# Two matmuls per head, from stacked high and low parts, in the second block's attention

## The chip, the cores and the metric

One Trainium2 chip, one core. The metric is device time in microseconds of the whole program, the median of several executions. PE is TensorE (matmuls), PEld its weight loads, DVE VectorE, ACT ScalarE, POOL GpSimd, SP the engine that issues most DMAs.

## What is computed

A first block (an MLA layer, an RG-LRU layer, each followed by a SwiGLU) on 272 tokens, then a second block of two layers on 256 tokens with model width 2048. The change touches only the attention of the second block. Each of its layers has 32 heads of 64 channels in four kinds of mixer, eight heads each, cut here to what matters:

```python
h = rms_norm_2(x, norm_gain[layer])
proj = jnp.einsum('bsd,dc->bsc', h, w_in[layer])          # q, k, v, gate, forget
o_a = dilated_attention(rope(norm(q[0])), rope(norm(k[0])), v[0])
o_b = stick_breaking_attention(q[1], k[1], v[1])
o_c = moba_attention(rope(norm(q[2])), rope(norm(k[2])), v[2])
o_d = forgetting_attention(norm(q[3]), norm(k[3]), v[3], log_f)
y = heads_side_by_side(o_a, o_b, o_c, o_d) * silu(gate)
x = x + jnp.einsum('bsc,cd->bsd', y, w_out[layer])
```

For each head this is: scores q.k over 256 queries and 256 keys (the upper triangle is masked out), a softmax or the stick-breaking weights, and the product of these weights with the values.

## The kernel before, in words

All matmuls take operands of type float32r. To keep float32 precision, an operand x is split into a high part (x cast to float32r on ACT) and a low part (x minus the high part, on DVE), and `mm3` (L225) makes a product of three matmuls: high by high, high by low, low by high. `wblock` (L206) does the same to each block of weights that a DMA on SP brings in (`wraw`): ACT casts `wh` (L216), DVE subtracts `wl` (L191). Several such blocks are in flight.

`block2` (L685) runs the four mixers of a layer in the order 1, 0, 2, 3. Per mixer there are four pairs of heads, i = 0 to 3. `values` (L714) projects v for two pairs at once; `qkg` (L738) projects q, k and the gate of one pair, and `qk` (L823) normalizes, rotates and splits q and k (channels of the pair's two heads on partitions 0 to 63 and 64 to 127, the 256 tokens as columns). `attend` (L759) does the attention of one pair, so it is called 16 times per layer, 32 times in all: 8 times with `stick` (L921) and 24 times with `soft` (L881). `out_proj` (L777) of the previous mixer is put between.

Both `soft` and `stick` work on two blocks of 128 queries (`lo`, `hi`). A matmul contracts over all 128 partitions, that is over both heads at once, so one of the two operands must be block-diagonal. `diag` (L871) copies a block of 128 columns into such a form, [head 0 | 0; 0 | head 1], 256 columns wide, into buffers that `diagpad` (L860) has zeroed once per layer; POOL copies the high part, DVE the low part, two casts each (L878). With it the scores of the first block take one `mm3` of 256 columns for both heads (L896 in `soft`, L931 in `stick`), those of the second one `mm3` of 256 columns for each head (L902, L930):

```python
qd = self.diag(q, hi)
kd = self.diag(k, lo)
self.mm3(s0[:, 0:256], (q[0][:, lo], q[1][:, lo]), kd, NC is None, True)
for j in range(2):
    s = s1[:, j * 256:j * 256 + 256]
    self.mm3(s, block(qd, j), (k[0][:, 0:256], k[1][:, 0:256]), NC is None, ...)
```

The value product (L767, L768) loads the values of both heads, 128 columns, and streams the attention weights of both heads, 512 columns for the first 128 keys and 256 for the others; of the result o (128 x 512) each head takes its own half of the partitions, multiplied by the gate (`yt`, L773), which is then split into `yh` (L774) and `yl`.

The order in which each engine does its work is set when the program is built, by the framework's scheduler from the data dependences and the program's order; PE fills waits of one attention with projections of another part. Tiles come from pools with a fixed number of buffers, 66 in the large pool "s".

Of the kernel before, what the change touches and what calls it, by code (L numbers as in the profile page):

```python
# [9 lines left out]
F32 = mybir.dt.float32  # L10
F32R = mybir.dt.float32r
# [43 lines left out]
def halves(x, n):  # L55
    return x.rearrange("p (j c) -> p j c", c=n)


def block(pair, j):
    return [t[:, j * 128:j * 128 + 128] for t in pair]  # L60

# [14 lines left out]
class Net:  # L76
# [608 lines left out]
    def block2(self, l, st, rb, first_done, after):  # L685
# [24 lines left out]
        NC = None  # L710
        self.diagpad(4)
        Y = {}

        def values(mx, hf):  # L714
            out = []
            ft = []
            c = 264 if mx == 3 and hf == 0 else 256
            src = a[f"vf{l}"] if c == 264 else a[f"v{l}"][(1, 0, 2, 3).index(mx) * 2 + hf - (mx == 3)]
            ws = [self.wblock(src[b], 8 * c, 4 * c) for b in range(2)]
            for tt in range(2):  # L720
                p = self.ps()[:, 0:c]
                ts = slice(tt * 128, tt * 128 + 128)
                for k in range(KD):
                    xh, xl = X[k]
                    self.mm3(p, (xh[:, ts], xl[:, ts]), self.wcol(ws[k // 8], (k % 8) * c, c), k == 0, k == KD - 1)
                if c == 264:
                    ft.append(self.small.tile([128, 8], F32, tag="ft", name="ft"))
                    nc.vector.tensor_scalar(ft[tt], p[:, 256:264], rcol()[:, tt:tt + 1], None, ALU.mult)
                p = p[:, sl]
                vh = self.slot("vh", F32R)[:, sl]  # L730
                vl = self.slot("vl", F32R)[:, sl]
                rc = rcol()[:, tt:tt + 1]
                nc.scalar.activation(vh, p, AF.Copy, scale=rc)  # L733
                nc.vector.scalar_tensor_tensor(vl, p, rc, vh.bitcast(F32), ALU.mult, ALU.subtract)
                out.append((vh, vl))
            return out, ft
# [22 lines left out]
        def attend(mx, i, q, k, g, v):  # L759
            o = self.pa("o2")  # L760
            c = slice((i % 2) * 128, (i % 2) * 128 + 128)
            hv = [[t[:, c] for t in x] for x in v]
            if mx == 1:
                p0, p1 = self.stick(q, k, masks)
            else:
                p0, p1 = self.soft(q, k, masks, NC if mx == 3 else None, i)
            self.mm3(o, hv[0], p0, True, False)  # L767
            self.mm3(halves(o, 256)[:, :, 128:256], hv[1], p1, False, True)  # L768
            yh, yl = Y[mx][i]
            t = self.slot("yt", tag="a")[:, sl]  # L770
            for j in range(2):
                R = slice(j * 64, j * 64 + 64)
                nc.vector.tensor_tensor(t[R], o[R, j * 256:j * 256 + 256], g[R], ALU.mult)  # L773
            nc.scalar.copy(yh, t)  # L774
# [48 lines left out]
    def qk(self, l, mx, qk, p, rb):  # L823
# [4 lines left out]
        if mx == 1:  # L828
            if qk == 0:
                nc.vector.scalar_tensor_tensor(t, p, 0.125, rb()[:, sl], ALU.mult, ALU.mult)  # L830
            else:
                nc.vector.tensor_tensor(t, p, rb()[:, sl], ALU.mult)
            return self.split(t, "qk", n)
        nc.vector.tensor_tensor(t, p, rb()[:, sl], ALU.mult)
# [21 lines left out]
        if mx == 3:  # L856
            return self.split(t, "qk", n)
        return self.rope(t, self.b2const["rope2c"], self.b2const["rope2s"], n, "qk", (v, y))

    def diagpad(self, n):  # L860

        self.dp = []
        self.dpi = 0
        for _ in range(n):
            pr = (self.slot("dph", F32R), self.slot("dpl", F32R))
            for t in pr:
                for j in range(2):
                    self.nc.gpsimd.memset(t[j * 64:j * 64 + 64, 128 - j * 128:256 - j * 128].bitcast(F32), 0.0)
            self.dp.append(pr)

    def diag(self, x, c):  # L871

        pr = self.dp[self.dpi % len(self.dp)]
        self.dpi += 1
        for t, s, eng in zip(pr, x, (self.nc.gpsimd, self.nc.vector)):
            for j in range(2):
                R = slice(j * 64, j * 64 + 64)
                eng.tensor_copy(t[R, j * 128:j * 128 + 128], s[R, c])  # L878
        return [t[:, 0:256] for t in pr]

    def soft(self, q, k, masks, NC, i):  # L881
# [3 lines left out]
        lo, hi = slice(0, 128), slice(128, 256)  # L885
        qd = self.diag(q, hi)
        kd = self.diag(k, lo)
        if NC is not None:
# [6 lines left out]
            nc.tensor.matmul(s1, self.one, nb, start=True, stop=False)  # L895
        self.mm3(s0[:, 0:256], (q[0][:, lo], q[1][:, lo]), kd, NC is None, True)  # L896
        P = []
        for j in range(2):
            P.append([self.softmax(s0[:, j * 128:j * 128 + 128], 128, 128, masks[0])])
        for j in range(2):  # L900
            s = s1[:, j * 256:j * 256 + 256]
            self.mm3(s, block(qd, j), (k[0][:, 0:256], k[1][:, 0:256]), NC is None, NC is None or j == 1)  # L902
        for j in range(2):
# [17 lines left out]
    def stick(self, q, k, masks):  # L921
# [4 lines left out]
        lo, hi = slice(0, 128), slice(128, 256)  # L926
        qd = self.diag(q, hi)
        kd = self.diag(k, lo)
        for j in range(2):
            self.mm3(z0[:, j * 256:j * 256 + 256], block(kd, j), (q[0][:, 0:256], q[1][:, 0:256]))  # L930
        self.mm3(z1[:, 0:256], (k[0][:, hi], k[1][:, hi]), qd)  # L931
        Z, SP = [], []
# [279 lines left out]
```

## Time and profile before

| | us |
|---|---|
| median of 3 executions | 3184.17 |
| lowest and highest | 3183.94, 3185.53 |
| profiled execution | 3183.68 |
| its span, from the first to the last instruction | 3181.9 |
| PE busy | 3159.5 |
| DVE busy | 2160.8 |
| ACT busy | 1758.9 |
| POOL busy | 588.9 |

A busy time is the union of the durations of an engine's instructions. Matmuls overlap, so what PE takes for one is read from the distance of the starts. In the rows a group is named by its line, its engine, its operation, what it writes and reads and the shapes; 128*128 is the size of the loaded weights, behind it stand the output's partitions and columns.

### The profile page before, as it was taken

Reading aid. Unit: us, or ns where it says so; the run is one execution under the profiler, and the core shown is the slowest. Engines: PE = TensorE matmul, PEld = TensorE weight load, DVE = VectorE, ACT = ScalarE, POOL = GpSimd, SP = SyncE. Lnnn points to the kernel's source line nnn. Section 1 sums busy time; section 2 is a strip of 40 time slices with the busy share of each in tenths; the row PEclk is TensorE's granted clock in tenths of the full one; section 3 lists DMA queues with packets and bytes.
Section 4 is the critical chain, followed back from the end, with each engine's and each line's share of the span. In section 5 each row is a group of like instructions: output and inputs, shape, how many; then the busy total and the mean of one; then the engine's idle time right before and its main releaser. Section 6 shows DMA issues by size and latency. Waiting matters only on the chain.

```text
span 3181.9 us, 64455 instructions
## 1 busy us (share of the span) xinstructions
PE 3159.5 (99%) x25987; PEld 3139.0 (99%) x25987; DVE 2160.8 (68%) x3673; ACT 1758.9 (55%) x2970; POOL 588.9 (19%) x730
## 2 busy tenths in 40 slices
PE   9999999999999999999999999999999999999999
PEld 9999999999999999999999999999999999999999
DVE  7887655555555678865555555578788778778876
ACT  6765434434344567754444444456677666666764
POOL 1001000000000134310000000023244463144453
PEclk9999999999999999999999999999999999999999
DMA  6344556556565555566565656556555555555554
GB/s 226 118 131 127 179 158 194 175 160 190 160 191 170 178 176 171 166 194 187 173 201 171 204 182 189 189 165 201 167 166 164 175 159 177 160 174 169 167 168 134
DMA packets 165693, 549.43 MB, mean 173 GB/s; under 512 B 18800, under 2 KB 38128, under 8 KB 165392
## 3 DMA queue, kind: packets, MB, share of 16 engines
q1 hardware_dynamic: 163440, 540.70, 54.6%
q8 instruction: 203, 3.33, 0.4%
q0 software_dynamic: 1664, 4.33, 0.4%
q14 instruction: 98, 0.80, 0.1%
q10 hardware_dynamic: 288, 0.27, 0.0%
HBM read 543.13 MB, written 2.10 MB: 171 GB/s over the span
## 4 chain that ended last, share of the span: by engine, by line
PE 83%; DVE 2%; issue 1%; DMA 1%; POOL 1%; ACT 1%; POOLq 0%; ACTq 0%; DVEq 0%; SPq 0%
PE p L230 27%; PE p L228 27%; PE p L229 27%; DVE wl L191 1%; DMA gw<-lru_gate 0%; DVE hs L606 0%; DMA wraw<-in 0%; DVE xc L624 0%; PE o L229 0%; PE o L230 0%; PE o L228 0%; ACT wh L216 0%; PE s L228 0%; PE s L230 0%; PE s L229 0%
## 5 line engine op out<-in xcount | busy, mean ns | idle before, releaser
L216 ACT CAST wh<-wraw 128x1024 fp32r<-128x1024 f32 (+3 forms) x1107 | 1087.8, 984 | 967.8 <-PE p L229 731.0
L191 DVE TENSOR_TENSOR wl<-wraw,wh 128x1024 fp32r<-128x1024 f32 (+3 forms) x1107 | 1292.3, 1168 | 334.7 <-issue 248.4
L228 PE MATMUL p<-xh,wh 128*128 128x256 f32 (+1 forms) x5040 | 1430.7, 284 | 0.2 <-DVE qkt L830 0.2
L229 PE MATMUL p<-xl,wh 128*128 128x256 f32 (+1 forms) x5040 | 1428.8, 283 | 1.3 <-DVE xl L256 1.3
L230 PE MATMUL p<-xh,wl 128*128 128x256 f32 (+1 forms) x5040 | 1428.4, 283 | 0.0
L229 PEld LDWEIGHTS p<-xl,wh 128*128 128x128 f32 x5040 | 950.1, 189 | 2.2 <-DVE xl L256 1.5
L228 PEld LDWEIGHTS p<-xh,wh 128*128 128x128 f32 x5040 | 949.2, 188 | 1.3 <-ACT vh L733 0.3
L230 PEld LDWEIGHTS p<-xh,wl 128*128 128x128 f32 x5040 | 948.6, 188 | 0.5
L229 PE MATMUL p<-hidl,wh 128*128 128x272 f32 (+1 forms) x1408 | 400.5, 284 | 0.0
L230 PE MATMUL p<-hidh,wl 128*128 128x272 f32 (+1 forms) x1408 | 400.4, 284 | 0.0
L228 PE MATMUL p<-hidh,wh 128*128 128x272 f32 (+1 forms) x1408 | 400.2, 284 | 0.0
L229 PEld LDWEIGHTS p<-hidl,wh 128*128 128x128 f32 x1408 | 265.5, 189 | 0.0
L230 PEld LDWEIGHTS p<-hidh,wl 128*128 128x128 f32 x1408 | 265.2, 188 | 0.0
L228 PEld LDWEIGHTS p<-hidh,wh 128*128 128x128 f32 x1408 | 265.1, 188 | 0.0
L269 POOL TENSOR_TENSOR acc<-acc,sq 128x256 f32<-128x256 f32 (+1 forms) x81 | 76.3, 942 | 990.9 <-ACT sq L268 902.0
L228 PE MATMUL p<-yh,wh 128*128 128x256 f32 x768 | 216.1, 283 | 0.0
L230 PE MATMUL p<-yh,wl 128*128 128x256 f32 x768 | 216.0, 282 | 0.0
L229 PE MATMUL p<-yl,wh 128*128 128x256 f32 x768 | 215.9, 281 | 0.0
L269 POOL TENSOR_TENSOR accf<-accf,sq 128x256 f32<-128x256 f32 x15 | 15.7, 1047 | 702.1 <-ACT sq L268 702.1
L229 PEld LDWEIGHTS p<-yl,wh 128*128 128x128 f32 x768 | 145.0, 189 | 0.1
L228 PEld LDWEIGHTS p<-yh,wh 128*128 128x128 f32 x768 | 144.6, 189 | 0.5
L230 PEld LDWEIGHTS p<-yh,wl 128*128 128x128 f32 x768 | 145.0, 189 | 0.0
(360 smaller groups left out, 4308.4 us busy)
## 6 DMA issues: line engine op xcount, KB each, us to landing
wraw<-gu SPq DMA_DIRECT2D x352, 512.0 KB, 3.9
wraw<-dn SPq DMA_DIRECT2D x128, 512.0 KB, 3.5
wraw<-in SPq DMA_DIRECT2D x128, 512.0 KB, 4.3
wraw<-lru_in SPq DMA_DIRECT2D x64, 512.0 KB, 3.7
wraw<-g SPq DMA_DIRECT2D x64, 512.0 KB, 3.7
wraw<-out SPq DMA_DIRECT2D x64, 512.0 KB, 3.7
wraw<-v SPq DMA_DIRECT2D x56, 512.0 KB, 4.0
wraw<-dn SPq DMA_DIRECT2D x128, 192.0 KB, 2.7
```

The costliest lines, as they stand in the source:

```text
L191: return self.nc.vector.tensor_tensor(out, x, h.bitcast(F32), ALU.subtract)
L216: nc.scalar.copy(h[:, 0:c], raw)
L228: nc.tensor.matmul(p, lh, rh, start=first, stop=False)
L229: nc.tensor.matmul(p, lh, rl, start=False, stop=False)
L230: self.last_mm = nc.tensor.matmul(p, ll, rh, start=False, stop=last)
L269: (eng or nc.gpsimd).tensor_tensor(st[key], st[key], s[:, 0:n], ALU.add)
```

## The change

q and k are no longer put into block-diagonal form for both heads. For each head j one operand is stacked, the high part on the head's own 64 partitions and the low part on the other 64 (`split_weights`, for the operand that is loaded), and the other holds the high part on both halves (`split_moving`), so that one matmul gives (high + low) by high. A second matmul adds high by low, from a copy of the high part with zeros in the other head's partitions (`hp`, zeroed by `halfpad`, copied on POOL). In `soft` q is loaded and k streams, in `stick` the other way round. The first block's scores now are two matmuls of 128 columns for each head, the second's two of 256 columns for each head.

The values of a head are kept as one loaded operand of 128 columns, high and low side by side, so that one matmul gives the product with the high values in one half of the partitions and that with the low values in the other half; it is done for the high and the low part of the attention weights. `attend` then adds the two halves: ACT copies one half out of PSUM into the other partitions (`ol`, in the large pool), DVE adds, and a further DVE instruction multiplies by the gate.

```diff
 def values(mx, hf):
-                vh = self.slot("vh", F32R)[:, sl]
-                vl = self.slot("vl", F32R)[:, sl]
                 rc = rcol()[:, tt:tt + 1]
-                nc.scalar.activation(vh, p, AF.Copy, scale=rc)
-                nc.vector.scalar_tensor_tensor(vl, p, rc, vh.bitcast(F32), ALU.mult, ALU.subtract)
-                out.append((vh, vl))
+                out.append([])
+                for i2 in range(2):
+                    v4 = halves(self.slot("vv", F32R)[:, sl], 64)
+                    vh, vl = v4[:, 0:4:3], v4[:, 1:3]
+                    pp = halves(p[:, i2 * 128:i2 * 128 + 128], 64)
+                    nc.scalar.activation(vh, pp, AF.Copy, scale=rc)
+                    nc.vector.scalar_tensor_tensor(vl, pp, rc, vh.bitcast(F32), ALU.mult, ALU.subtract)
+                    out[-1].append(v4)
 def attend(mx, i, q, k, g, v):
-            self.mm3(o, hv[0], p0, True, False)
-            self.mm3(halves(o, 256)[:, :, 128:256], hv[1], p1, False, True)
+            for j in range(2):
+                w0, w1 = (x[:, 2 * j:2 * j + 2].rearrange("p u c -> p (u c)") for x in hv)
+                oj = o[:, j * 256:j * 256 + 256]
+                for x in range(2):
+                    nc.tensor.matmul(oj, w0, p0[x][:, j * 256:j * 256 + 256], start=x == 0, stop=False)
+                for x in range(2):
+                    nc.tensor.matmul(oj[:, 128:256], w1, p1[x][:, j * 128:j * 128 + 128], start=False, stop=x == 1)
...
+            ol = self.slot("ol")[:, sl]
             for j in range(2):
-                R = slice(j * 64, j * 64 + 64)
-                nc.vector.tensor_tensor(t[R], o[R, j * 256:j * 256 + 256], g[R], ALU.mult)
+                R, L = slice(j * 64, j * 64 + 64), slice(64 - j * 64, 128 - j * 64)
+                oj = o[:, j * 256:j * 256 + 256]
+                nc.scalar.copy(ol[R], oj[L])
+                nc.vector.tensor_tensor(t[R], oj[R], ol[R], ALU.add)
+            nc.vector.tensor_tensor(t, t, g, ALU.mult)
 def qk(...):
-            return self.split(t, "qk", n)
+            return (self.split_moving if qk == 0 else self.split_weights)(t, "qk", n)
+        split = self.split_weights if qk == 0 else self.split_moving
+    def halfpad(self, n):
+        self.hp = []
         for _ in range(n):
+            pr = [self.slot("hp", F32R) for _ in range(2)]
+            for j, t in enumerate(pr):
+                self.nc.gpsimd.memset(t[64 - j * 64:128 - j * 64].bitcast(F32), 0.0)
+            self.hp.append(pr)
+    def split_weights(self, x, name, n):
+        st, hp = [], self.hp.pop(0)
+        self.hp.append(hp)
+        for j in range(2):
+            R, L = slice(j * 64, j * 64 + 64), slice(64 - j * 64, 128 - j * 64)
+            t = self.slot(name + "s", F32R)[:, 0:n]
+            nc.scalar.copy(t[R], x[R])
+            self.sub(t[L], x[R], t[R])
+            nc.gpsimd.tensor_copy(hp[j][R, 0:n], t[R])
+            st.append(t)
+        return st, hp
+    def split_moving(self, x, name, n):
+        tw = []
+        l = self.slot(name + "l", F32R)[:, 0:n]
+        for j in range(2):
+            R, L = slice(j * 64, j * 64 + 64), slice(64 - j * 64, 128 - j * 64)
+            t = self.slot(name + "t", F32R)[:, 0:n]
+            nc.scalar.copy(t[R], x[R])
+            self.sub(l[R], x[R], t[R])
+            nc.scalar.copy(t[L], x[R])
+            tw.append(t)
+        return tw, l
+    def heads(self, p, w, m, j, wc, mc, first, last):
+        nc.tensor.matmul(p, w[0][j][:, wc], m[0][j][:, mc], start=first, stop=False)
+        nc.tensor.matmul(p, w[1][j][:, wc], m[1][:, mc], start=False, stop=last)
 def soft(self, q, k, masks, NC, i):
-        qd = self.diag(q, hi)
-        kd = self.diag(k, lo)
-        self.mm3(s0[:, 0:256], (q[0][:, lo], q[1][:, lo]), kd, NC is None, True)
+        for j in range(2):
+            self.heads(s0[:, j * 128:j * 128 + 128], q, k, j, lo, lo, NC is None, NC is None or j == 1)
...
-            self.mm3(s, block(qd, j), (k[0][:, 0:256], k[1][:, 0:256]), NC is None, NC is None or j == 1)
+            self.heads(s, q, k, j, hi, slice(0, 256), NC is None, NC is None or j == 1)
 def stick(self, q, k, masks):
-        qd = self.diag(q, hi)
-        kd = self.diag(k, lo)
         for j in range(2):
-            self.mm3(z0[:, j * 256:j * 256 + 256], block(kd, j), (q[0][:, 0:256], q[1][:, 0:256]))
-        self.mm3(z1[:, 0:256], (k[0][:, hi], k[1][:, hi]), qd)
+            self.heads(z0[:, j * 256:j * 256 + 256], k, q, j, lo, slice(0, 256), True, True)
+        for j in range(2):
+            self.heads(z1[:, j * 128:j * 128 + 128], k, q, j, hi, hi, True, True)
```

`diagpad(4)` becomes `halfpad(2)`; `diagpad`, `diag` and `block` go.

## Rows read from the trace of the kernel before

**Rows 1.** The page: its span, PE's busy time, the chain by engine.
```profile
span 3181.9 us, 64455 instructions
...
PE 3159.5 (99%) x25987; PEld 3139.0 (99%) x25987; DVE 2160.8 (68%) x3673; ACT 1758.9 (55%) x2970; POOL 588.9 (19%) x730
...
PE 83%; DVE 2%; issue 1%; DMA 1%; POOL 1%; ACT 1%; POOLq 0%; ACTq 0%; DVEq 0%; SPq 0%
```

**Rows 2.** Busy time by stretch (us, instructions), second block: granted clock, DMA share, GB/s last.
```profile
2166.00:3182.00 1016.00, 1010.20 (x8420) 1002.98 (x8419) 803.98 (x1578) 671.19 (x1323) 399.62 (x518) 1.00 0.53 166
```

**Rows 3.** Timeline of PE (start us, duration us), scores of one call of soft.
```profile
2307.08 0.28 PE L228 MATMUL s<-qkh,dph 128*128 128x256 f32 x1
...
2307.79 0.28 PE L229 MATMUL p<-xl,wh 128*128 128x256 f32 x1
```

**Rows 4.** The same view, value product of the last call.
```profile
3156.16 0.39 PE L230 MATMUL o<-p,vl 128*128 128x512 f32 x1
3156.39 0.28 PE L228 MATMUL o<-p,vh 128*128 128x256 f32 x1
```

**Rows 5.** Groups of PE by line and shape, whole span: count, busy us, mean ns.
```profile
L229 PE MATMUL s<-qkl,dph 128*128 128x256 f32 x48 | 13.5, 280 | 0.0
...
L229 PE MATMUL o<-p,vh 128*128 128x512 f32 x32 | 12.6, 395 | 0.0
...
L229 PE MATMUL o<-p,vh 128*128 128x256 f32 x32 | 9.0, 281 | 0.0
```

**Rows 6.** Timeline of weight loads in the first block, behind 16-column matmuls.
```profile
79.46 0.19 PEld L229 LDWEIGHTS s<-kl,qh 128*128 128x128 f32 x1
79.57 0.19 PEld L230 LDWEIGHTS s<-kh,ql 128*128 128x128 f32 x1
```

**Rows 7.** The same view, transposes of the last call (128 columns).
```profile
3150.18 0.14 PEld L910 LDWEIGHTS s<-ident,e 128*128 128x128 f32 x1
...
3150.72 0.19 PEld L229 LDWEIGHTS p<-yl,wh 128*128 128x128 f32 x1
```

**Rows 8.** The same view, a plain float32 matmul of 256 columns (L1040).
```profile
2166.75 0.30 PEld L1040 LDWEIGHTS ms<-acc,ones 128*128 128x128 f32 x2
2167.08 0.19 PEld L229 LDWEIGHTS p<-wl,xh 128*128 128x128 f32 x1
2167.29 0.19 PEld L230 LDWEIGHTS p<-wh,xl 128*128 128x128 f32 x1
```

**Rows 9.** Timeline of PE in the first block: four matmuls of 16 columns, then another.
```profile
79.37 0.17 PE L229 MATMUL s<-kl,qh 128*16 128x16 f32 x1
...
79.48 0.37 PE L229 MATMUL s<-kl,qh 128*128 128x256 f32 x1
```

**Rows 10.** Groups of ACT, DVE and POOL by line and shape, second block.
```profile
L463 ACT COPY hry<-qkt 32x256 f32<-32x256 f32 x128 | 51.7, 404 | 47.2 <-DVE qkt L855 45.8
L733 ACT ACTIVATE vh<-p,rc 128x256 fp32r<-128x256 f32 x32 | 14.5, 467 | 5.8 <-PE p L230 3.9 <-DVE rc L983 1.4 <-DVE ft L728 0.5
L197 ACT CAST qkh<-qkt 128x256 fp32r<-128x256 f32 x32 | 12.8, 402 | 11.9 <-DVE qkt L855 10.3 <-DVE qkt L832 1.7
...
L878 DVE CAST dpl<-qkl 64x128 fp32r<-64x128 f32 x128 | 36.5, 285 | 1.6
L773 DVE TENSOR_TENSOR yt<-o,gt 64x256 f32<-64x256 f32 x64 | 27.0, 421 | 18.6 <-PE o L230 18.0
...
L878 POOL CAST dph<-qkh 64x128 fp32r<-64x128 f32 x128 | 65.4, 511 | 174.1 <-ACT qkh L197 170.2
```

**Rows 11.** Who waited for whom, second block: us in total, times, longest.
```profile
ACT wh L216 <- PE p L229: 104.3, 95, 2.7
```

**Rows 12.** Timeline of ACT and of weight loads, the last call's end.
```profile
3157.91 0.41 ACT L774 CAST yh<-yt 128x256 fp32r<-128x256 f32 x1 [2.87 <-DVE yt L773]
...
3159.15 0.54 PEld L228 LDWEIGHTS p<-yh,wh 128*128 128x128 f32 x4
```

More of the change, by code (lines that the diff above doesn't have):

```diff
@@ L56, in halves @@
     return x.rearrange("p (j c) -> p j c", c=n)
-def block(pair, j):
-    return [t[:, j * 128:j * 128 + 128] for t in pair]
 class Lazy:
@@ L710, in block2 @@
         NC = None
-        self.diagpad(4)
+        self.halfpad(2)
         Y = {}
@@ L760, in attend @@
             o = self.pa("o2")
-            c = slice((i % 2) * 128, (i % 2) * 128 + 128)
-            hv = [[t[:, c] for t in x] for x in v]
+            hv = [x[i % 2] for x in v]
             if mx == 1:
@@ L856, in qk @@
         if mx == 3:
[L857 to L863, printed above, removed]
-        for _ in range(n):
[L865 to L879, printed above, removed]
+            return split(t, "qk", n)
+        return self.rope(t, self.b2const["rope2c"], self.b2const["rope2s"], n, "qk", (v, y), split)
@@ new lines, in halfpad @@
+    def halfpad(self, n):
+        self.hp = []
+        for _ in range(n):
+            pr = [self.slot("hp", F32R) for _ in range(2)]
[3 more added lines that the diff above has]
+    def split_weights(self, x, name, n):
+        nc = self.nc
+        st, hp = [], self.hp.pop(0)
[8 more added lines that the diff above has]
+        return st, hp
@@ new lines, in split_moving @@
+    def split_moving(self, x, name, n):
+        nc = self.nc
+        tw = []
[9 more added lines that the diff above has]
+    def heads(self, p, w, m, j, wc, mc, first, last):
+        nc = self.nc
+        nc.tensor.matmul(p, w[0][j][:, wc], m[0][j][:, mc], start=first, stop=False)
+        nc.tensor.matmul(p, w[1][j][:, wc], m[1][:, mc], start=False, stop=last)
```

## The prediction

> **What bounds the kernel now.** I read the page's busy times first, then its chain. PE has work for 99% of the span, DVE for 68%, ACT for 55%, and PE holds 83% of the chain that ended last [rows 1]. A busy PE is not yet a PE at its peak, so the next view is the stretch that the change touches, the second block, from 2166 us to the end: PE is busy for 1010.2 of its 1016 us at a granted clock of 1.00, which is the 2.4 GHz level; DVE has work for 804 us, ACT for 671, POOL for 400 [rows 2]. In this stretch PE waits for almost nobody, so the time is the number of matmuls times the pace at which PE takes them, and an instruction saved on PE is time saved, as long as no other engine falls behind.
>
> The pace is read from starts, not from durations, since matmuls overlap. In one score step six matmuls of 256 columns start between 2307.08 and 2307.79 us [rows 3]: 0.71 / 6 = 0.118 us each. A matmul of 512 columns holds PE for 0.23 us [rows 4].
>
> **PE work removed and added.** One call of attend treats two heads. The value product runs three times per call, and each of its three groups has 32 rows [rows 5], so there are 32 calls. Per call the old form has nine score matmuls of 256 columns (three for the block kd or z1, twice three for the heads; 24 calls of soft give the 48 rows of one of these groups [rows 5]), three value matmuls of 512 and three of 256:
> 12 x 0.118 + 3 x 0.23 = 2.106 us.
>
> The new form has eight score matmuls (two heads x two blocks x two), four of 256 columns and four of 128, and eight value matmuls, four of 256 and four of 128. Every one loads 128 columns of weights, also where the same weights stand twice in a row. So PE gets 16 matmuls a call in place of 15, and a third fewer columns. Transposes, the NC matmuls, the projections and every DMA stay as they were; no queue gets more or fewer transfers.
>
> **The price that is not shown.** The trace of before has no matmul of the float32r type between 16 and 256 columns, so the 128-column one must be bounded.
> - From below: if only columns counted, 128 of them at 0.118 / 256 would take 0.059 us.
> - From the weights: a weight load of 128 columns that follows 16-column matmuls starts at 79.46, the one behind it at 79.57 [rows 6], so loads are 0.11 us apart even where PE has next to nothing to stream. The nearest rows in shape are the transposes, 128 columns with 128 columns of weights: their loads start at 3150.18 and, five later, at 3150.72 [rows 7], 0.108 us each.
> - From above: plain float32 matmuls need two passes, and a pass of 256 columns takes 0.21 to 0.22 us (loads at 2167.08 and 2167.29 [rows 8]); two of these per 256 columns are 1.68 ns a column, so 128 columns would cost 0.215 us, if a narrow float32r matmul were done at the rate of plain float32. The 16-column matmuls don't exclude that: they start 0.11 / 4 = 0.027 us apart [rows 9], and 16 x 1.68 ns is 0.027 as well; but that may be a floor on issuing any matmul.
>
> I take 0.108, the row nearest in shape. The new form then costs 8 x 0.118 + 8 x 0.108 = 1.808 us, 0.298 less per call, 9.5 us less in 32 calls.
>
> The Trainium skill (TensorE: Matmul & The Clock Gate, "Back-to-back issue gap") says that pairs of load and matmul at 128 columns go at about 81 ns each; the loads seen here are 0.11 us apart. An estimate by that page's figure would be 8 x 0.118 + 8 x 0.081 = 1.592, or 16.4 us saved in all.
>
> **Work on the other engines.** ACT's time goes by columns and hardly by partitions: 0.404 us for 32 x 256, 0.402 for 128 x 256 [rows 10]. So halving the partitions saves nothing and each half costs a whole. ACT loses two casts per call (the high parts of q and k) and gains two in split_weights, four in split_moving and two copies out of PSUM in attend; the value casts become two smaller ones in place of one, some 0.15 us more (an estimate: each smaller one at two thirds of today's 0.467). That is some +2.5 us a call, +81 us in all: 671 becomes 752 of 1016. DVE loses two subtractions and four casts of diag (0.285 each) and gains four half subtractions, one more product (0.421 each for 64 partitions) and a little for the values: about +0.2 us a call, +7 in all. POOL loses four casts of 0.51 [rows 10] for two wider ones, which is less work, and the memsets at a layer's start are fewer.
>
> All three stay below 81% of the stretch, so I price this at nothing by itself; the cover is the idle time in which ACT already waits for PE to release weight buffers, 104.3 us in this stretch [rows 11]. If that cover went, PE would wait for wh casts.
>
> Latency matters where PE has little else. The scores' chain hardly grows: a cast, a subtraction and two casts of diag in turn become four ACT copies of 0.4 with the subtractions beside them. Behind the value product it does: two products (0.84 us [rows 10]) become copy, copy beside add, add, product, 0.4 + 0.4 + 0.42 + 0.42 plus hand-overs, about 1 us more. At the end the cast yh is done at 3158.32, and the four loads that first need it start at 3159.15 [rows 12], 0.8 us later. So some 0.2 us shows, once per layer. Added waits: the ACT copy of ol waits for PE's last value matmul, and the weight casts queued behind it on ACT wait with it; DVE's first add waits for ACT where its product waited for PE alone. halfpad has two pairs in rotation, enough for two calls, as diagpad's four were. Bounds for all of this: nothing, and 4 us (one matmul's time, 0.12, lost in each of 32 calls). I take 1.5 us, nearer to nothing since ACT waits for PE and not the other way round.
>
> **Sum.** The profiled execution took 3183.68 us (span 3181.9 and 1.8 around it), 0.5 under the median of 3184.17. 3183.7 - 9.5 + 1.5 = 3175.7 us, 0.27% below the median. A measurement of this kernel can tell about 0.2% from no change, that is 6.4 us.
>
> **Rivals.**
> 1. Slower: the narrow matmul costs 0.215, as plain float32 does. Then a call takes 8 x 0.118 + 8 x 0.215 = 2.664, 0.558 more than now; 32 calls give +17.9 and with the 1.5 us **3203.1**. It decides from a price of (2.106 - 0.944) / 8 = 0.145 us upwards: above that the change loses. For it: nothing between 16 and 256 columns was ever run here, and the 16-column rows fit this price [rows 9]. Against it: the transposes at 0.108, and that a 16-column float32r matmul is one instruction where plain float32 shows two loads [rows 8, 9].
> 2. The gain is eaten: ACT's 81 us and the longer chains make PE wait. From 0.30 us of waiting per call nothing is left, **about 3182**. For it: DVE at 79% and ACT at 74% serve in order, and weight casts queue behind the copies. Against it: PE waits only 5.8 us in this stretch today [rows 2].
> 3. Columns alone count: 8 x 0.118 + 8 x 0.059 = 1.416, 22.1 saved, **3163.1**. Against it: loads 0.108 to 0.11 apart [rows 6, 7]. By the page's 81 ns the result would lie between this and mine, an estimate of 3168.8.
>
> **Chances.** My forecast 0.50, with its own range 3172 to 3180 (0 to 4 us of waits, and 2 us for an order of instructions that comes out differently). Rival 1 has 0.34, since its price is bounded and not excluded; rival 2 0.11; rival 3 0.05. Faster by over 0.2%: 0.40 of my case (in the rest the waits take it above 3177.8) and all of rival 3, 0.45. Within 0.2%: 0.09 of mine, 0.08 of rival 2, 0.17. Slower: rival 1, the bad part of rival 2 and 0.01 of mine, 0.38. The range must reach across both signs, since no one case has 0.8: 3170 to 3206, which holds nearly all of my case, rival 2 and most of rival 1, and leaves out rival 3.
>
> **What would show it.** In the timeline of PE, two 128-column matmuls in a row with starts 0.108 apart, or 0.215, or less than 0.1: this single number separates my case from rivals 1 and 3. The count of matmuls should be 25987 + 32. The second block's stretch should shrink by some 8 us and everything ahead of it stay. ACT's busy time there should rise by about 80 us, DVE's by under 15, POOL's fall. If the narrow pace is 0.108 and the time doesn't fall, rival 2 holds, and PE's rows must show idle time before score or value matmuls, released by ACT or DVE. I am wrong in the main step if the pace is above 0.145, and in the cover if PE idles over 10 us in this stretch.

## The result and the profile after

The change is slower: 3203.27 us, median of 6 executions (3201.26 to 3204.74), against 3184.82 us of the kernel before measured beside it. The ratio is 1.0057, 95% interval 1.0047 to 1.0067. The forecast was 3175.7 us and faster, with a range to 3206. That 3203.27 falls on the 3203.1 of rival 1 is chance: its mechanism, a narrow matmul at 0.215 us, is not there, as the loads below show. The profiled execution took 3201.26 us.

The page of the changed kernel, to be held against [rows 1]:

```profile
span 3199.5 us, 64690 instructions
...
PE 3159.7 (99%) x26019; PEld 3141.0 (98%) x26019; DVE 2180.0 (68%) x3673; ACT 1838.3 (57%) x3194; POOL 544.7 (17%) x642
...
PE 80%; DVE 4%; ACT 2%; POOL 2%; issue 1%; DMA 1%; POOLq 0%; ACTq 0%; DVEq 0%; SPq 0%
```

The count of matmuls is 25987 + 32, as forecast. ACT has 79 us more work, POOL 44 less. Now busy time by stretch, the columns of [rows 2]: the second block, and two stretches of 20 us in it.

```profile
2166.00:3199.50 1033.50, 1011.22 (x8457) 1006.40 (x8456) 823.44 (x1578) 749.52 (x1547) 354.40 (x432) 0.99 0.52 164
...
2290.00:2310.00 20.00, 13.60 (x93) 12.87 (x92) 15.47 (x29) 15.32 (x37) 9.19 (x13) 0.83 0.35 106
2650.00:2670.00 20.00, 17.27 (x125) 17.13 (x124) 13.11 (x23) 10.34 (x21) 3.48 (x4) 0.83 0.41 128
```

The stretch is 17.5 us longer than in [rows 2]. PE idles 1033.50 - 1011.22 = 22.3 us in it, where it idled 5.8. Its busy time did not fall by the expected 9.5 us either, it rose by 1.0. The two short stretches show why: around 2300 us PE idles 6.4 us of 20, and the granted clock falls to 0.83. The kernel before, the same view of the same 20 us:

```profile
2290.00:2310.00 20.00, 20.00 (x172) 20.00 (x171) 15.70 (x29) 13.55 (x29) 10.98 (x13) 1.00 0.58 174
```

There it did 172 matmuls, now 93. At 0.118 us each the missing 79 are 9.3 us, an estimate, of which 6.4 are idle time and 2.9 the lower clock. Who PE waited for in the second block of the changed kernel (us in total, times, longest):

```profile
PE p L224 <- DVE vv L733: 8.0, 3, 3.9
PE p L224 <- ACT yh L781: 5.5, 2, 2.7
PE o L769 <- ACT p L946: 1.2, 1, 1.2
```

The largest entry of the same view for the kernel before:

```profile
PE p L230 <- DVE xl L256: 0.6, 2, 0.3
```

So two kinds of wait are new, one for the value casts (vv) and one for the last yh of each layer. The weight loads of the changed kernel show the narrow pace, and what happens behind a long wait:

```profile
2304.40 0.29 PEld L224 LDWEIGHTS p<-xh,wh 128*128 128x128 f32 x1 [3.99 <-DVE vv L733]
2304.57 0.34 PEld L225 LDWEIGHTS p<-xl,wh 128*128 128x128 f32 x1
2304.78 0.33 PEld L226 LDWEIGHTS p<-xh,wl 128*128 128x128 f32 x1
...
2305.85 0.33 PEld L225 LDWEIGHTS p<-xl,wh 128*128 128x128 f32 x1
...
2405.41 0.19 PEld L909 LDWEIGHTS s<-qkl,hp 128*128 128x128 f32 x1
2405.52 0.19 PEld L908 LDWEIGHTS s<-qkt,qks 128*128 128x128 f32 x1
2405.63 0.30 PEld L909 LDWEIGHTS s<-qkl,hp 128*128 128x128 f32 x2
2405.85 0.19 PEld L908 LDWEIGHTS s<-qkt,qks 128*128 128x128 f32 x1
```

The loads from 2405.41 belong to four score matmuls of 128 columns; the fifth follows at 2405.85, so they are 0.11 us apart. That is the 0.108 of the forecast. Behind the wait that ends at 2304.40 ordinary matmuls of 256 columns start 0.213 us apart (six steps from 2304.57 to 2305.85), not 0.118: PE runs at the 1.2 GHz level there (granted clock 0.50, row in the last section).

What the first kind of wait is can be followed on PE and ACT. Timeline of PE, then of ACT:

```profile
2270.24 0.28 PE L226 MATMUL p<-wh,xl 128*128 128x256 f32 x1
...
2300.22 0.33 PE L771 MATMUL o<-p,vv 128*128 128x128 f32 x2
2304.40 0.58 PE L224 MATMUL p<-xh,wh 128*128 128x256 f32 x1 [3.85 <-DVE vv L733]
...
3173.68 0.33 PE L771 MATMUL o<-p,vv 128*128 128x128 f32 x2
3176.75 0.74 PE L224 MATMUL p<-yh,wh 128*128 128x256 f32 x4 [2.73 <-ACT yh L781]
```

```profile
2297.76 1.05 ACT L212 CAST wh<-wraw 128x1024 fp32r<-128x1024 f32 x1
2300.59 0.37 ACT L778 COPY ol<-o 64x256 f32<-64x256 f32 x1 [1.78 <-PE o L771]
2300.98 0.37 ACT L732 ACTIVATE vv<-p,rc 128x128 fp32r<-128x128 f32 x1
...
2303.46 0.63 ACT L732 ACTIVATE vv<-p,rc 128x128 fp32r<-128x128 f32 x2
2304.64 0.37 ACT L732 ACTIVATE vv<-p,rc 128x128 fp32r<-128x128 f32 x1 [0.55 <-DVE vv L733]
...
3174.05 0.37 ACT L778 COPY ol<-o 64x256 f32<-64x256 f32 x1 [4.15 <-PE o L771]
3174.90 0.36 ACT L778 COPY ol<-o 64x256 f32<-64x256 f32 x1 [0.48 <-DVE yt L779]
3176.29 0.40 ACT L781 CAST yh<-yt 128x256 fp32r<-128x256 f32 x1 [1.02 <-DVE yt L780]
```

The value projections of the next two pairs were done on PE at 2270 us. ACT casts them 30 us later, from 2300.98 on, right behind ol, the first copy of the fold (the copies and adds behind the value product), which had to wait for that product on PE. Meanwhile their sums occupy accumulators, and PE's next projection (p) waits until DVE has subtracted vv. It is the same all over the second block: at each of the 14 places where the program names value casts behind a copy ol, the first cast starts 0.4 us after the start of such a copy. The second kind of wait is the end of a layer: PE has nothing to do from its last value product until yh, and the fold is a chain of 3176.69 - 3174.05 = 2.64 us in which copy, add, copy, add follow each other. The kernel before, timeline of DVE at the same place:

```profile
3157.02 0.86 DVE L773 TENSOR_TENSOR yt<-o,gt 64x256 f32<-64x256 f32 x2 [1.11 <-PE o L230]
```

From the start of its two products to the end of the cast yh [rows 12] it took 3158.32 - 3157.02 = 1.30 us, and PE had other matmuls behind its last value product until 3159.15 [rows 4, 12].

### The profile page after: what moved, and what is told of

Same layout as the page of the kernel before. It is cut to its first block, busy times and chain, and to the rows that moved or that the text cites. A ratio compares the mean times of both kernels' runs of the same rounds, so it can differ in the third digit from the quotient of the medians.

```text
span 3199.5 us, 64690 instructions
## 1 busy us (share of the span) xinstructions
PE 3159.7 (99%) x26019; PEld 3141.0 (98%) x26019; DVE 2180.0 (68%) x3673; ACT 1838.3 (57%) x3194; POOL 544.7 (17%) x642
## 4 chain that ended last, share of the span: by engine, by line
PE 80%; DVE 4%; ACT 2%; POOL 2%; issue 1%; DMA 1%; POOLq 0%; ACTq 0%; DVEq 0%; SPq 0%
PE p L224 26%; PE p L226 26%; PE p L225 26%; DVE wl L187 1%; ACT wh L212 1%; PE o L769 0%; DVE hs L602 0%; POOL nb L920 0%; POOL hrt L858 0%; DVE xc L620 0%; DMA gw<-lru_gate 0%; POOL hrt L860 0%; PE s L909 0%; PE s L908 0%; PE o L771 0%
## 5 line engine op out<-in xcount | busy, mean ns | idle before, releaser
L226 PE MATMUL p<-wh,xl 128*128 128x256 f32 (+1 forms) x512 | 144.4, 283 | 0.5 <-DVE xl L252 0.5
```

What stands on the lines that cost most here:

```text
L226: self.last_mm = nc.tensor.matmul(p, ll, rh, start=False, stop=last)
```

## The experiments

Every ratio is against the kernel before on the same chip (3184.69 to 3185.29 us), with its 95% interval. Differences between variants are differences of medians, often from different chips, between which the kernel before itself moves by 0.6 us. The theories: **F**, the longer fold behind the value product; **S**, the new splits of q and k; **V**, the value casts, two small ones in place of a wide one.

**Halves of the change.** First the new scores with the old values and product.

```diff
-                w0, w1 = (x[:, 2 * j:2 * j + 2].rearrange("p u c -> p (u c)") for x in hv)
...
+            self.mm3(o, hv[0], p0, True, False)
+            self.mm3(halves(o, 256)[:, :, 128:256], hv[1], p1, False, True)
```

> The new scores with the old value product and the old value casts. Theory F (the fold): the loss sits in attend's end, where ACT copies half of o out of PSUM, DVE adds, and value casts queue behind the copies; then this kernel has none of it and keeps the scores' saving of about 0.158 us a call, 5 us in all: 3178 to 3182, PE hardly waiting in the second block. Theory S (the split): ACT's six half casts per call and their latency are the loss; then it stays above 3192. Theory V (the value casts in four alternating steps hold the PSUM tile of the projection too long): as F, 3178 to 3182.

Measured 3183.44 us, 0.9996 (0.9986 to 1.0005), no single wait of PE in the second block above 0.6 us. S falls. The score half does no harm, but of the 5 us that it should bring only 1.2 show, which is within the noise, and the time is above the range of F and V. Where the rest went was not followed. Then the other half, the old scores with the new value casts, product and fold:

```diff
-            self.heads(s0[:, j * 128:j * 128 + 128], q, k, j, lo, lo, NC is None, NC is None or j == 1)
+        self.mm3(s0[:, 0:256], (q[0][:, lo], q[1][:, lo]), kd, NC is None, True)
...
-            self.heads(s, q, k, j, hi, slice(0, 256), NC is None, NC is None or j == 1)
+            self.mm3(s, block(qd, j), (k[0][:, 0:256], k[1][:, 0:256]), NC is None, NC is None or j == 1)
```

> The old scores with the new value product, its value casts and its fold. F and V: all of the loss is here, and the scores' saving of 5 us is missing: 3200 to 3210. S: the values' saving alone, 3178 to 3182.

3197.71 us, 1.0041 (1.0026 to 1.0056), with 5.5 us of waits for yh and 4.7 for vv. The loss is in the value half, though less than F and V wanted. The two halves (1.2 us faster, 12.9 slower) don't add up to the 18.4 us of the whole change. Then the fold dropped from the change:

```diff
-                nc.scalar.copy(ol[R], oj[L])
-                nc.vector.tensor_tensor(t[R], oj[R], ol[R], ALU.add)
-            nc.vector.tensor_tensor(t, t, g, ALU.mult)
+                nc.vector.tensor_tensor(t[R], oj[R], g[R], ALU.mult)
```

> The changed kernel without the copy and the add: each head's half of o goes straight into the product with the gate, two DVE instructions as before the change. This leaves the product with the low parts of the values out of the result. PE's work is the same. F: the loss is gone, 3173 to 3179. S or V: at least 3192.

3184.19 us, 0.9999 (0.999 to 1.0009). PE's only large wait:

```profile
PE p L224 <- ACT yh L778: 2.9, 2, 1.5
```

The waits for vv are gone although no value cast was touched. But the time is above what F wanted.

**Whole casts.** One ACT and one DVE cast per value projection, into four tiles of 512 columns of their own; the large pool shrinks to 58 to make room:

```diff
-SLOTS = {"s": 66, ...}
+SLOTS = {"s": 58, ..., "v": 4}
...
-                    v4 = halves(self.slot("vv", F32R)[:, sl], 64)
...
+                vv = self.slot("vv", F32R, [128, 512], "v")
...
```

> The changed kernel with each projection of values cast in one ACT and one DVE instruction into a tile of 512 columns (a pool of four such tiles; the large pool has 58 in place of 66), where the change has two of each. V: the loss goes, 3173 to 3182. F: the fold and its order stay, 3195 or more. S: no difference, about 3203.

3190.6 us, 1.0018 (1.0008 to 1.0027). Again no waits for vv, so both F's and V's expectations are half met. The first block became 7 us longer, with a granted clock of 0.87 between 130 and 175 us (1.00 in the kernel before): with 58 tiles, which must hold the zero padding too, that block is short of them, as a later run bears out.

**Four attempts on the order.** High priority for the value casts (theory Q, the queue order), both copies ahead of the adds, the old product for each layer's last pair (theory T, the tail), and all three at once.

```diff
-                for i2 in range(2):
+                with self.tc.high_priority(HP):
+                    for i2 in range(2):
...
+                        nc.scalar.activation(vh, pp, AF.Copy, scale=rc)
```

> The changed kernel with the value casts (ACT and DVE) given a high priority, so that they are put into their queues as soon as their projection is done, ahead of the copies of o. The same instructions. Theory Q: neither the fold nor the value casts are dear by themselves; PE's waits of 3 to 4 us come where value casts stand in ACT's queue behind a copy of o that waits for PE or DVE, so that no PSUM tile is free for the next projection, and the clock falls behind them. Then PE's 8.0 us of waits for vv go, with the half-clock stretches at 2297 and 2819 us: 3186 to 3192. Theory F (the fold's own time): within 3 us of 3203.

3201.26 us, 1.0052 (1.0037 to 1.0067), the same waits to a tenth: a miss.

```diff
-                nc.scalar.copy(ol[R], oj[L])
...
+                nc.scalar.copy(ol[R], o[L, j * 256:j * 256 + 256])
+            for j in range(2):
...
```

> The changed kernel with both copies of o ahead of both adds, so that the second copy doesn't wait for the first add. The same instructions. F with the alternation of ACT and DVE as the cost: the chain gets about 0.5 us shorter in each call and the waits shrink, 3190 to 3197. Q: the copies still stand before value casts and wait for PE, 3199 to 3203.

3204.51 us, 1.0057 (1.004 to 1.0074), 12.1 us of waits for vv: a miss.

```diff
+            old = (mx, i) == (3, 3)
+            if old:
...
+                self.mm3(o, hl[0], p0, True, False)
+                self.mm3(halves(o, 256)[:, :, 128:256], hl[1], p1, False, True)
...
```

> The changed kernel, with the last pair of each layer alone done in the old way (three matmuls for both heads, gate applied out of PSUM, no fold). A second theory, T: at a layer's end PE has nothing left but work on this pair, so its chain from o to yh shows in full; PE waited there twice for 2.7 us for yh. T: those go, with the half clock at 2656 us: 3194 to 3198. If only Q matters: 3201 or more.

3200.68 us, 1.0049 (1.0034 to 1.0064): the waits for yh fall from 5.5 to 2.9 us, those for vv stay, at 9.3. T's range is missed, though the waits that it named are halved.

The three edits together:

> The edits of the three runs above together. Q and T as the whole cause: PE's saving is left, 3175 to 3181. If something else eats it too (no run so far fell clearly below the kernel before): 3182 to 3187.

3205.43 us, 1.0064 (1.0049 to 1.0079), 12.0 us of waits for vv: a miss, outside both ranges. Neither the priority nor the fold's own order helps.

**Where the value tiles come from.** New theory P: the large pool is full, so the casts wait for a free tile.

```diff
-SLOTS = {"s": 66, ...}
+SLOTS = {"s": 58, ..., "v": 8}
...
-                    v4 = halves(self.slot("vv", F32R)[:, sl], 64)
+                    v4 = halves(self.slot("vv", F32R, tag="v")[:, sl], 64)
```

> The changed kernel with one thing moved: the value operands take eight tiles of a small pool of their own (with the six zero-padding tiles of the first block, which are dead by then), and the large pool shrinks from 66 to 58 tiles. The number of instructions, the halved casts and the fold stay. Theory P (the value casts wait for a tile of the full large pool, PE then finds no free accumulator): PE's waits for the value cast of VectorE (8.0 us in three) go to under 1 us, the two for yh (5.5 us) stay, and the time is 3185 to 3192. Theory F (the fold chain alone): 3198 to 3204, the value waits stay. Theory V (too many small value casts): 3197 to 3204, the same.

3187.68 us, 1.001 (1.0001 to 1.002): 15.6 us back, no waits for vv, those for yh (5.5) as they were. As P said, with the number of tiles unchanged at 66. But any theory by which vv waits for something in the large pool would have said the same.

Then the whole casts of above, with the zero padding of the first block in the four wide tiles:

```diff
-            pr = (self.slot("zph", F32R), self.slot("zpl", F32R))
+            z = self.slot("zp", F32R, [128, 512], "v")
+            pr = (z[:, 0:256], z[:, 256:512])
```

> The earlier run with one ACT and one VectorE cast for each value projection, with its first block mended: the zero-padding pairs lie in the value pool's four wide tiles, so that the large pool of 58 serves the rest. The fold stays. Theories P and V both: no value waits, the first block as long as in the kernel before (the second block starts near 2159 us), 3182 to 3187. If the first block stays 7 us longer, the large pool of 58 is too small there whatever the padding does, and the time is 3189 to 3192.

3183.12 us, 0.9995 (0.9986 to 1.0005), the first block as before. Against the run with halved casts the whole ones are 4.6 us faster. Last for P, more tiles in the shared pool:

```diff
-SLOTS = {"s": 66, ...}
-WB = (4, 6, 5)
+SLOTS = {"s": 70, ...}
+WB = (3, 6, 5)
```

> The changed kernel with four more tiles in the large pool (70 in place of 66), paid for by one raw weight buffer less of four in one of the weight queues. Nothing else is changed. Theory P: PE's waits for value casts fall from 8.0 us to under 3 us, the time is 3186 to 3195 unless the missing weight buffer brings waits for weights, which would be named as waits for weight casts or DMA queues. Theories F and V: value waits as in the change, 3199 to 3205.

3231.41 us, 1.0146 (1.0131 to 1.0161). There are two readings. The missing raw weight buffer costs time all over, seen as ACT's waits in the second block:

```profile
ACT wh L212 <- DMA wraw<-g: 38.4, 34, 3.3
ACT wh L212 <- DMA wraw<-in: 32.8, 31, 3.1
```

And against P, PE's waits for vv did not fall: 10.6 us, with four tiles more. That speaks against a full pool, though the missing weight buffer disturbs this run. The order of ACT's instructions as built, of the change, shows what stands ahead of vv (numbers count tiles in the order in which the program names them):

```
1670 L778 COPY ol_27234<-o2_27172 64x256 [waits PE_49]
1671 L732 ACTIVATE vv_27319<-p_27270,rc_26598 128x2x64
1672 L778 COPY ol_27234<-o2_27172 64x256 [waits DVE_49]
1673 L732 ACTIVATE vv_27322<-p_27270,rc_26598 128x2x64 [waits DVE_49]
```

At this place some 45 of the 66 tiles are in use, counted from the addresses and last uses in the built program: the pool is not full. (It is the place at 2243 us of the trace; at 2300 us the casts stand behind ol in the same way.) The tile ol is named just ahead of vv, in the same pool. Theory O: the pool gives tiles out in the order in which the program names them, so that a vv can't be written before ol is, and ol waits for PE's value product.

**What eats the rest.** L: the gaps at the layers' ends are on the path; C: PE's work was the cover of other chains, and what is freed there is waited for elsewhere. First the whole casts in their pool, with the old product for each layer's last pair (the two edits above):

> The run with whole casts in a pool of their own, and each layer's last pair of heads with the value product of the kernel before (six matmuls, no copy and add). Theory L (the two waits behind the last fold, 1.0 us each by name, and gaps of 1.4 us on PE, are on the path): 2 to 2.5 us less than without this, 3180 to 3181.5, the waits for yh gone. Theory C (PE's work was the cover of the other engines' chains, whatever is freed in one place is waited for in another): 3182 to 3184.

3178.8 us, 0.9981 (0.9972 to 0.999), below even L's range and faster than both kernels, with the wait for yh gone; it is 4.3 us faster than the run without the old tail. PE in it, the end of the last layer:

```profile
3152.40 0.28 PE L227 MATMUL o<-p,vv 128*128 128x256 f32 x1
3152.52 0.28 PE L225 MATMUL p<-yh,wh 128*128 128x256 f32 x1
```

Behind its last value product PE goes on with output matmuls of earlier pairs, while yh is made (ACT's cast starts at 3153.68). Then the kernel before with less work on PE and nothing else changed:

```diff
-            self.mm3(o, hv[0], p0, True, False)
...
+            nc.tensor.matmul(o, hv[0][0], p0[0], start=True, stop=False)
+            nc.tensor.matmul(o, hv[0][0], p0[1], start=False, stop=False)
```

(and the same for the second block of keys.)

> The kernel before with less work on PE and no other engine's work changed: the product of the values' low part with the high weights is left out (of each call one matmul of 512 and one of 256 columns, 0.232 and 0.118 us, 11.2 us in 32 calls). If a saving on PE shows when nothing is added elsewhere (theory L): 3173 to 3176. If other engines' chains set the pace wherever PE gets faster (theory C): 3179 to 3184, with new waits of PE under 1 us each for ACT, DVE and POOL.

3173.93 us, 0.9964 (0.9952 to 0.9977): 11.2 us faster, just what was taken out.

```profile
2166.00:3171.00 1005.00, 999.27 (x8364) 993.99 (x8362) 801.22 (x1578) 669.37 (x1323) 410.55 (x520) 1.00 0.52 168
```

PE's busy time falls by 10.9 us against [rows 2] and its idle time stays at 5.7. C falls as a general rule: a saving on PE is a saving of time, as long as nobody else is made later.

Third the whole casts without the fold (both edits stand above):

> The run with whole casts in a pool of their own, without copy and add: the product takes the output's own half, so that of each head one half of the value product is left out. Theory L (the fold is what remains): 3175 to 3179. Theory C: 3180 to 3184, with PE's named waits for yh gone and small waits elsewhere.

3180.45 us, 0.9986 (0.9977 to 0.9994): above L's range and inside C's, whose small waits are there (1.6 us for the sums h). Leaving the fold out of all calls brings 2.7 us here, where leaving it out of each layer's last call, with the old product there, brought 4.3. So the two are not one cost added up call by call: what PE is given to do around them differs too.

**The decisive word.** In the change, ol from yt's pool:

```diff
-            ol = self.slot("ol")[:, sl]
+            ol = self.slot("ol", tag="a")[:, sl]
```

> The changed kernel with one word changed: the tile ol of the fold comes from the pool that yt is in, no longer from the large pool that also holds the value operands. The large pool keeps 66 tiles; no instruction is added or removed. Theory O (tiles of one pool are given out in the order in which the program names them, so value operands named behind ol can't be written ahead of ol's copy, which waits for PE's value product): the value casts run well ahead of that copy, PE's waits for vv (8.0 us in three) are under 1 us, the waits for yh (5.5 us) stay, 3185 to 3191. Theory P (the pool is too full): one tile less in 66 is nothing, the waits stay, 3198 to 3204.

3188.04 us, 1.001 (1.0001 to 1.0019): 15.2 us back with no instruction added or removed. ACT's timeline and PE's 20 us around 2300:

```profile
2268.33 0.36 ACT L732 ACTIVATE vv<-p,rc 128x128 fp32r<-128x128 f32 x1
...
2276.92 0.36 ACT L732 ACTIVATE vv<-p,rc 128x128 fp32r<-128x128 f32 x1
2282.32 0.37 ACT L778 COPY ol<-o 64x256 f32<-64x256 f32 x1 [0.36 <-PE o L771]
```

```profile
2290.00:2310.00 20.00, 20.00 (x171) 20.00 (x170) 14.11 (x19) 13.87 (x27) 11.05 (x10) 1.00 0.52 165
```

The four casts run 5 to 14 us ahead of the copy, PE does 171 matmuls where it did 93, and the clock stays at 1.00. What PE still waits for:

```profile
PE p L224 <- ACT yh L781: 5.5, 2, 2.7
```

O holds, P falls. At all 14 places the casts now start ahead of the copy that is named before them. The other runs agree: PE waits 4.7 to 12.1 us for vv in each of the seven kernels in which ol and vv come from one pool, and no wait for vv is named in the nine others that have vv. Last, the same edit in two other kernels, first the fastest one.

> The fastest variant so far (whole value casts in a pool of their own, the old value product for each layer's last pair) with ol in yt's pool as well. Theory O: there ol still stood in one pool with the next call's query and key operands, which are named behind it; if they were held up by it, 1 to 4 us come free, 3175 to 3178. If they were not (they are not ready ahead of the copy anyway): 3178 to 3180, the same as without.

3186.65 us, 1.0006 (0.9998 to 1.0015): 7.9 us slower than without it, a miss on both counts. PE's waits and its end of the last layer:

```profile
PE p L225 <- ACT yh L796: 2.9, 2, 1.5
PE hms L867 <- POOL qsql L864: 2.5, 4, 0.8
```

```profile
3161.39 0.28 PE L227 MATMUL o<-p,vv 128*128 128x256 f32 x1
3163.12 0.62 PE L225 MATMUL p<-yh,wh 128*128 128x256 f32 x3 [1.46 <-ACT yh L796]
```

The value product is the old one here, with no fold, and PE waits 1.5 us all the same, for here the scheduler has put the last value product right ahead of the matmuls that need yh, and nothing between. These two waits are 2.9 us; in the whole second block PE idles 12.9 us here and 6.0 in the fastest variant. So the wait at a layer's end is the length of the chain less what the built order leaves for PE behind it, and the order differs from kernel to kernel.

Then the change with ol moved and the old product for each layer's last pair:

> The changed kernel with ol in yt's pool and the old value product for each layer's last pair; the value casts stay halved and in the large pool. Theory O with the tail's two waits on the path: 2 to 5 us less than with ol moved alone, 3181 to 3186, PE's waits for yh gone or under 3 us. Against the fastest variant the distance is then the price of the halved casts (3 to 6 us). If the value waits come back in another place: above 3190.

3185.59 us, 1.0001 (0.9992 to 1.001): 2.5 us less than with ol alone, the waits for yh 2.9 us. Both are as expected. The distance to the fastest variant is 6.8 us, above the 3 to 6 that were to be the price of the halved casts.

## Why the prediction was wrong

**PE work removed: right.** The narrow pace is 0.11 us, where 0.108 was taken. Rival 1 (0.215) and rival 3 (0.059) fall by the same loads. By the distances of starts in the second block, a matmul of 128 columns costs 0.110 us in a row of its kind and some 0.115 alone between wider ones, and one of 512 columns 0.231, so a call saves some 0.27 us and 32 calls some 8.5 us, an estimate (9.5 forecast). That such a saving reaches the end was shown by taking 11.2 us out of the kernel before. The Trainium skill (TensorE: Matmul & The Clock Gate, "Back-to-back issue gap") gives 81 ns at 128 columns and 131 at 512; the trace does not agree, with 110 and 231.

**Work on the other engines: right for ACT and POOL, too low for DVE, and not the cause.** ACT rose by 78 us in the second block (80 forecast), POOL fell by 45. DVE rose by 19 where 7 was forecast and under 15 named as the sign; the halved value subtractions alone are 2 x 0.345 us in place of 0.480 in each call. PE's large waits were not for `wh` or `wl`. The cover of [rows 11] held: ACT still waits 54.1 us for PE to release weight buffers.

**Latency and added waits, "I take 1.5 us", bounds nothing and 4 us: this is the step that failed.** With 8.5 us saved and 18.4 lost, the waits and what hangs on them are worth 27 us. In the profiled runs 16.5 us of this are more idle time of PE, the rest is a longer busy time, slow stretches among it. The reason given for 1.5, that ACT waits for PE and not the other way round, was the error: where ACT waits for PE with a copy of ol (25.4 us in 14 waits), the value casts behind that copy wait too, and then PE waits for them. The loss comes in three parts.
- *What waits behind the copy of ol.* The prediction saw that this copy waits for PE's last value matmul and named the weight casts behind it. What mattered were the value casts of the next pairs, which share ol's pool and are named behind it. Moving ol took 15.2 us away, moving the casts' tiles 15.6. The three waits named for vv are 8.0 us of that; the rest is put down to shorter waits and the lower clock behind them; it was not added up. The kernel before had no such tile, since yt comes from another pool.
- *The end of a layer.* The fold was taken as 1 us longer; it is 1.34. But the slack of 0.8 us [rows 12] was taken as fixed. It is a matter of the built order, and in the changed kernel there is none, so the whole chain shows: 2.7 us in each layer where 0.2 was taken. With the old product in each layer's last pair, 2.5 us (halved casts) and 4.3 us (whole casts) came back; how much of each is chain and how much order was not separated.
- *The halved value casts.* They were taken as 0.15 us more per call on ACT, each at two thirds of a whole cast, and this was priced at nothing. They take 0.365 us each against 0.467 for a whole one, so 0.26 more. Whole casts in their own pool are 4.6 us faster than halved ones in theirs. That the casts' own time is the reason, and not the order that came out, was argued and not shown.

Bounding the waits by "one matmul's time lost in each of 32 calls" was the error of method. About half of the loss, 13.5 us, sat in five waits of 1.3 to 3.9 us, and behind three of these in stretches at the lower clock; the number of calls says nothing about those.

**The rivals.** Rival 2, the gain eaten by waits, had the mechanism, with 0.11 and a time of 3182; it had no term for more than the saving itself. At 0.84 us of waiting per call (27 / 32), against its threshold of 0.30, it ends on the slower side. The 0.38 for slower rested almost wholly on rival 1. The sign named in the text for being wrong in the cover, PE idle over 10 us in this stretch, is there: 22.3.

**What stays open.** The best variant keeps 6.3 of some 8 us. The same word, ol's pool, makes that variant 7.9 us slower and the change 15.2 us faster, although no instruction is added or removed, so several us here hang on the order that is built. Why the scheduler chose either order was not followed. The word also puts one tile more per call into yt's pool of ten, from which the next calls' attention weights come; whether this made that variant slower, no run tells.

## What to carry to other kernels

When a step gets a new temporary tile, look at which tiles its pool gives out next, and to whom: a tile written only late holds back all that is named behind it in that pool, however many tiles are free and whatever their priority. Give a tile that waits for the end of a chain a pool in which nothing else is urgent, and measure it: the same move cost 7.9 us in one variant here. And price the last call of a layer by itself: behind it there may be nothing to hide the chain, and a slack read from one built order is not a property of the kernel.

## What the runs showed of the hardware

A wait of PE can cost more than its length. Behind the wait of 3.85 us at 2304.40 matmuls started 0.213 us apart for a while in place of 0.118, the 1.2 GHz level in place of 2.4, and the 20 us around it had a mean granted clock of 0.83: by the estimate above 2.9 us on top of 6.4 idle. It does not follow every wait. Of the five longest in the changed kernel's second block, the granted clock fell behind those that ended at 2304.40, 2660.95 (2.73 us) and 2822.7 (2.81 us), and stayed at 1.00 behind the one at 3176.75, which was 2.73 us long as well, and the shortest (1.32 us). What tells the two of 2.73 us apart was not followed. Stretches behind the longest four, in order of time, with the columns of [rows 2]:

```profile
2304.60:2308.00 3.40, 3.40 (x17) 3.40 (x18) 3.29 (x10) 3.21 (x9) 0.85 (x2) 0.50 0.00 0
2661.40:2666.60 5.20, 5.20 (x26) 5.20 (x26) 3.96 (x7) 3.75 (x8) 0.66 (x1) 0.50 0.17 35
2824.00:2827.00 3.00, 3.00 (x16) 3.00 (x15) 2.12 (x5) 1.51 (x5) 1.49 (x3) 0.50 0.06 20
3176.75:3180.00 3.25, 3.25 (x26) 3.24 (x27) 2.65 (x6) 2.00 (x2) 0.00 (x0) 1.00 0.25 80
```

The core's mean granted clock was 0.997 in the change and 1.000 in the fastest variant, whose longest named wait in the second block is 0.6 us. And a raw weight buffer is worth far more here than four tiles: with three buffers in place of four, and four tiles more, the kernel lost 28 us against the change, with ACT waiting for the weights' DMAs.
